# Four down stages of a two-layer hybrid block: product 4 copied by ScalarE with an adding DMA, squares added by DMAs, the short stage's weights loaded and split sooner

## The chip, the cores and the metric

The kernel runs on one core of a Trainium2 chip. Its engines each work through their own list of instructions in order: TensorE (PE, matrix products), VectorE (DVE), ScalarE (ACT), GpSimd (POOL) and SyncE (SP, which here only issues DMAs). POOL and ACT issue DMAs too. An instruction waits at the head of its engine's list until semaphores say that its operands are there. The metric is the device time of one execution in microseconds (us), as the median of several runs. The profile is of one execution, and its span is a little shorter than that execution's device time.

## The reference

Two layers of a hybrid transformer over 1024 tokens of width 1024, in float32. Layer 0 mixes tokens by a bidirectional retention (four heads, 256 context tokens ahead), layer 1 by a gated convolution of width 3. Each is followed by a SwiGLU feed-forward layer (hidden width 2816):

```python
hx = hx + g1 * yx                       # yx: retention or convolution, ends in a matmul by w_out
fx = modulate(rms_norm(hx, norm_ffn[i]), sh2, sc2)
hx = hx + g2 * swiglu(fx, ffn_w1[i], ffn_w3[i], ffn_w2[i])
...
return rms_norm(hx, final_norm)
```

Shifts, scales and gates (`sh`, `sc`, `g`) come from the conditioning vector. So each of the four sub-layers ends in the same pattern: a matrix product back to width 1024 (here called a down stage), times a gate, added to the residual stream `hx`, and then the root mean square of the new `hx` over its 1024 channels, which scales the input of what follows.

## The kernel before

Activations lie with channels on the 128 partitions: the stream is 8 channel tiles (`kt` 0 to 7) by 2 token blocks (`tb`) of 512 tokens, each a tile of 128x512. TensorE multiplies with a rounded operand type, so each operand is split in a high and a low part: `split` lets ScalarE copy and round (L132, or L127 with a sign) and VectorE subtract (L133, L128), and `mm3` makes three matmuls of it (L137, L138, L139).

The large products use Winograd's form of Strassen's algorithm: operands in 2x2 blocks, seven products instead of eight. A down stage, made by `down`, runs its seven products in the order 1, 5, 6, 3, 7, 4, 2. Each product is `nh` units, one for each pair of hidden tiles, and each unit is 4 output tiles by 3 matmuls. The stages are A (`o_run`, the retention's output, nh 8), B (first FFN, nh 11), C (the convolution's output, nh 4, called the short stage) and D (last FFN, nh 11, which also makes the final result).

- **Operands.** `operands(m)` runs three units ahead: it loads one tile of activations (L1110, from `x_d` in DRAM, where the stage before stored it), splits it, forms the weight sum of this product and splits that. `w_load` (L1090) loads half a weight tile on SP's queue; `w_add` (L1094) adds two weight tiles by an accumulating DMA on POOL's queue. First halves are loaded ahead of the stage, second halves in product 1, unit by unit.
- **Results.** At the end of a product, `finished` calls `update` for each of its 4 tiles. For products 1, 5 and 6 (`D_FIRST`), ScalarE copies the sum with the gate (L1142) and an accumulating DMA of POOL adds the residual (L1143). For products 3, 7, 4 and 2 VectorE adds to the tile that is there (L1146). `D_OUT` says which tile and token block a product belongs to; product 4 gives tiles 4 to 7 of the first block, to which `load_h` has loaded the residual on SP's queue (L1135) at the start of product 7.
- **Norm.** `complete` squares each finished tile (ScalarE, L1165 for a block's first, L264 for others), adds the square to the block's sum (VectorE, L265), and stores the tile for the next residual (L1169). `norm_steps` then gives the list of small pieces: `rstd` (TensorE's L270 sums over partitions, VectorE's chain L275 to L155 takes the reciprocal root), L288 puts it on a diagonal, L296 on TensorE spreads it, and the next stage's tiles are scaled by it (L1301).
- **Order.** `hooks` is a queue of small pieces of work. After each unit `unit_done` takes one or two out and runs them, so that their instructions land between units; `nothing` is an empty piece that ends the turn. The second block's norm is queued at the start of product 4 and the first block's at the stage's end, so that its steps run between the first units of the stage that follows.
- **Last stage.** In D, product 2 does its 256 first tokens, keeps the operands and does the other 256 after. ScalarE scales finished tiles by the final gain (L1415, `result_tile`) and TensorE turns them (L1409, `result_turn`).

A scheduler places instructions on each engine from this program's order, and pools of buffers (`up`, `tp`, `lp` and 8 PSUM banks) decide when a load or a copy may begin.

Of the kernel before, what the change touches and what calls it, by code (L numbers as in the profile page):

```python
# [14 lines left out]
AF = mybir.ActivationFunctionType  # L15
ALU = mybir.AluOpType
# [7 lines left out]
KT = D // P  # L24
# [28 lines left out]
def hybrid_kernel(ctx: ExitStack, tc: tile.TileContext, a: dict):  # L53
    nc = tc.nc
# [18 lines left out]
    def ttile():  # L73
        return tp.tile([P, 512], F32, tag="t", name="tt")
# [12 lines left out]
    def ttile2():  # L87
        return extra["l"].tile([P, 512], F32, tag="l", name="t2")
# [17 lines left out]
    hooks = deque()  # L106
# [115 lines left out]
    def until(ready):  # L222
        while not ready():
            hooks.popleft()()
# [82 lines left out]
    def in_parts(src):  # L307
        u = unit()
        split(u[:, 0], u[:, 1], src)
        return u  # L310
# [754 lines left out]
    H = {}  # L1065
# [5 lines left out]
    D_AHEAD = 3  # L1071
# [1 line left out]
    LATER = slice(0, TB // 2), slice(TB // 2, TB)  # L1073
    D_LOADS = 3

    D_FIRST = (1, 5, 6)

    def down(src, nh, w, gate, residual, order, consume, then=(), last=False):

# [6 lines left out]
        def w_load(k, half):  # L1086
            if k not in wr:
                wr[k] = raw()
            c = slice(half * 512, (half + 1) * 512)
            nc.sync.dma_start(wr[k][:, c], w[k][:, c])  # L1090

        def w_add(i):

            nc.gpsimd.dma_start(wr[i][:, 512:], w[nh + i][:, 512:], accum_op=ALU.add)  # L1094

        loaded = [0]

# [15 lines left out]
        def operands(m):  # L1113
            x_loads(m + 1, True)
            x_loads(m + 1 + D_LOADS)
            if m >= len(seq):
                return
            n, i = seq[m]
            xs[m] = in_parts(xl.pop(m))
            wa, wc = wr[i][:, :512], wr[i][:, 512:]  # L1120
            if n != 1:
                wb, wd = wr[nh + i][:, :512], wr[nh + i][:, 512:]
            if n == 6:
                nc.vector.tensor_sub(wc, wc, wa)
            if n in (3, 7):
                t = ttile()
                nc.vector.tensor_sub(t, wb if n == 3 else wd, wc)
            else:
                t = wa if n == 1 else {5: wc, 6: wc, 2: wb, 4: wd}[n]
            ws[m] = in_parts(t)  # L1130

        def load_h():
            for kt in range(4, KT):
                H[kt, order[0]] = ttile2()
                nc.sync.dma_start(H[kt, order[0]], residual(kt, order[0]))  # L1135

        def update(n, kt, tb, ps, t):

# [9 lines left out]
        def norm_steps(tb):  # L1148
            box = {}

            def diag():
                box["dg"] = rstd_diag(accs[tb], TB)

            def bank_of(i, step):
                if i == 0:
                    box["rb"] = spread(box["dg"], TB)
                step(box["rb"])

            return [diag, nothing] + [lambda i=i, f=f: bank_of(i, f) for i, f in enumerate(consume(tb))]

        def complete(kt, tb, t):
            h = H[kt, tb]
            if tb not in accs:
                accs[tb] = ttile()
                nc.scalar.activation(accs[tb], h, AF.Square)  # L1165
            else:
                sq_add(accs[tb][:, t], h[:, t], False, t.stop - t.start)
            if not last:
                nc.scalar.dma_start(h_d[kt][tb], h)  # L1169

        ahead = [lambda i=i: w_load(i, 0) for i in range(nh)]
        ahead[3:3] = [lambda: x_loads(D_LOADS)]
        ahead += [lambda m=m: operands(m) for m in range(D_AHEAD)]

        def step(ps, c, w, x, t, first, end):
            k = slice(c * P, (c + 1) * P)
# [2 lines left out]
        def run():  # L1179
            banks, kept = {}, []  # L1180

            def finished(n, c, ps, t):
                j, r = D_OUT[n]
                kt, tb = 4 * j + c, order[r]
                update(n, kt, tb, ps, t)
                if n in (3, 7, 2, 4):
                    complete(kt, tb, t)
                if last and n in (2, 4):
                    result_tile(kt, t)

            for m, (n, i) in enumerate(seq):
                which = "A" if n in (1, 6, 7, 4) else "B"
                if i == 0:
                    if n == 7:
                        load_h()
                    if n == 5:
                        until(lambda: src(2, nh - 1) is not None)
                    if n in (1, 5, 2):
                        banks[which] = [bank() for _ in range(4)]
                    if n == 4:  # L1200
                        hooks.extend(then[:1])
                        hooks.extend(norm_steps(order[1]))
                        hooks.extend(then[1:])
                    if n == 2 and last:
                        hooks.extend(
                            lambda kt=kt: result_turn(kt, LATER[0]) for kt in range(4, KT)
                        )
                if n == 1:
                    w_load(i, 1)
                    w_load(nh + i, 1)  # L1210
                    w_add(i)
                if n == 6:
                    w_load(nh + i, 0)
                until(lambda: m in ws)
                operands(m + D_AHEAD)
                w, x = ws.pop(m), xs.pop(m)
                t = TOKENS
                if last and n == 2:
                    kept.append((w, x))
                    t = LATER[0]  # L1220
                for c in range(4):
                    step(banks[which][c], c, w, x, t, n in (1, 5, 2) and i == 0, i == nh - 1)
                if i == nh - 1:
                    for c in range(4):
                        finished(n, c, banks[which][c], t)
                unit_done(2 if n in (1, 2, 4) or nh == 4 else 1)
            if last:
                flush()
                acc = accs[order[0]]
                for c in range(4):  # L1230
                    ps = bank()
                    for i, (w, x) in enumerate(kept):
                        step(ps, c, w, x, LATER[1], i == 0, i == nh - 1)
                    finished(2, c, ps, LATER[1])
                    if c == 0:
                        for kt in range(4):
                            result_turn(kt, LATER[0])
                        y = result_norm(acc, LATER[0])
                    if c == 1:
                        result_end(y, LATER[0])  # L1240
                        for kt in range(4, KT):
                            result_turn(kt, LATER[1])
                    if c > 1:
                        result_turn(c - 2, LATER[1])
                y = result_norm(acc, LATER[1])
                for c in (2, 3):
                    result_turn(c, LATER[1])
                result_end(y, LATER[1])
            else:
                hooks.extend(norm_steps(order[0]))  # L1250
# [398 lines left out]
```

## Time and profile before

| | us |
|---|---|
| median of 3 runs | 2626.91 (2619.53 to 2627.34) |
| profiled execution | 2628.3 |
| its span | 2626.4 |
| PE busy | 2565.5 (98%) |
| DVE busy | 1889.3 (72%) |
| ACT busy | 1235.6 (47%) |
| POOL busy | 323.7 (12%) |
| mean granted TensorE clock | 0.992 |

A row of a timeline gives start, duration, engine, line, operation, output and input, and in brackets how long the engine stood idle before it and what ended that. A row of a window gives its bounds and length, TensorE's busy time (and instructions), the granted clock (1.00 is full), the DMA engines' share and GB/s. A row of waits gives total, times and longest. Rows of one line give minimum, median and maximum in ns, and first and last start. A matmul's duration overlaps the next one's, so their pace is the distance between starts. Part 6 of the page gives, for each kind of DMA, the count, its size and the median time from issue to landing.

### The profile page before, as it was taken

The page shows a single profiled execution, that of the slowest core. Times are in us where ns is not written, and L with a number is a line of the kernel's source. Part 1 is how long each engine was busy: PE and PEld are TensorE (multiplying, and loading weights), DVE is VectorE, ACT ScalarE, POOL GpSimd, SP SyncE. Part 2 cuts the span into 40 slices and gives each one's busy share as a digit, 9 for nine tenths or more (in the row PEclk, how much of TensorE's full clock was granted, in tenths as well). Part 3 has the DMA queues.
Part 4 walks back from the last instruction along what each step waited for, and adds up shares of the span by engine and source line. Part 5 has one row for each costly group of instructions (what it writes and reads, how often), then busy time and mean ns, then how long its engine had stood idle before and what let it go on. Part 6 is the DMA issues. An engine that isn't in the chain of part 4 may idle for free.

```text
span 2626.4 us, 33369 instructions
## 1 busy us (share of the span) xinstructions
PE 2565.5 (98%) x11508; PEld 2099.9 (80%) x11508; DVE 1889.3 (72%) x3333; ACT 1235.6 (47%) x2239; POOL 323.7 (12%) x370
## 2 busy tenths in 40 slices
PE   8999999999989999999999999999999999999998
PEld 4788888887777787888887888788777888887888
DVE  4886766767887867777776767777688666655766
ACT  4653232447776545433333545533366333333544
POOL 1100222002332102000001100200112000002100
PEclk9999999999999999999999999999999999999999
DMA  9546233764569957444556945432685333329733
GB/s 328 203 149 220 92 124 128 260 216 132 182 217 279 272 157 161 135 157 153 181 187 214 276 138 172 91 100 98 181 240 103 117 104 112 109 89 299 199 88 117
DMA packets 218985, 445.12 MB, mean 169 GB/s; under 512 B 23104, under 2 KB 52928, under 8 KB 218816
## 3 DMA queue, kind: packets, MB, share of 16 engines
q1 hardware_dynamic: 149232, 297.94, 35.4%
q0 software_dynamic: 32864, 79.19, 12.4%
q10 hardware_dynamic: 36720, 65.86, 6.7%
q8 instruction: 91, 1.49, 0.2%
q14 instruction: 78, 0.64, 0.1%
HBM read 320.74 MB, written 109.58 MB: 164 GB/s over the span
## 4 chain that ended last, share of the span: by engine, by line
PE 86%; DVE 6%; DMA 5%; issue 2%; ACT 1%; SPq 0%; DVEq 0%; ACTq 0%
PE ps L137 28%; PE ps L138 28%; PE ps L139 27%; DVE u L133 2%; PE ps L237 1%; DMA tt<-x_d 1%; DMA tt<-os_d 1%; DMA tt<-g_d 1%; DVE u L675 1%; PE ps L947 0%; DVE kh L634 0%; PE ps L296 0%; DMA raw<-in_w_g 0%; DVE tt L265 0%; PE ps L270 0%
## 5 line engine op out<-in xcount | busy, mean ns | idle before, releaser
L137 PE MATMUL ps<-u 128*128 128x512 f32 (+1 forms) x3492 | 1363.7, 391 | 17.9 <-DVE u L133 8.5
L138 PE MATMUL ps<-u 128*128 128x512 f32 (+1 forms) x3492 | 1356.7, 389 | 2.1 <-DVE u L133 1.9
L139 PE MATMUL ps<-u 128*128 128x512 f32 (+1 forms) x3492 | 1355.9, 389 | 0.0
L137 PEld LDWEIGHTS ps<-u 128*128 128x128 f32 x3492 | 659.1, 189 | 162.5 <-ACT u L132 10.0
L138 PEld LDWEIGHTS ps<-u 128*128 128x128 f32 x3492 | 659.7, 189 | 137.7 <-DVE u L133 4.7
L139 PEld LDWEIGHTS ps<-u 128*128 128x128 f32 x3492 | 659.4, 189 | 135.1 <-issue 0.7
L132 ACT CAST u<-raw 128x512 fp32r<-128x512 f32 x622 | 375.5, 619 | 379.9 <-PE ps L139 234.3
L133 DVE TENSOR_TENSOR u<-raw,u 128x512 fp32r<-128x512 f32 x622 | 434.8, 711 | 60.2 <-ACT u L132 59.4
L133 DVE TENSOR_TENSOR u<-tt,u 128x512 fp32r<-128x512 f32 x358 | 242.2, 700 | 123.4 <-ACT u L132 121.4
L132 ACT CAST u<-tt 128x512 fp32r<-128x512 f32 x358 | 211.9, 620 | 206.0 <-DMA tt<-x_d 102.4
L443 ACT COPY tt<-ps 128x512 f32<-128x512 f32 x192 | 112.6, 587 | 251.8 <-PE ps L139 244.5
L128 DVE SCALAR_TENSOR_TENSOR u<-raw,u 128x512 fp32r<-128x512 f32 x168 | 114.9, 688 | 76.6 <-ACT u L127 76.4
L127 ACT ACTIVATE u<-raw 128x512 fp32r<-128x512 f32 x168 | 105.1, 632 | 88.2 <-PE ps L139 75.8
L1263 POOL DMA_DIRECT2D x_d<-tt x52 | 28.3, 544 | 837.6 <-DVE tt L1276 774.2
L456 DVE TENSOR_TENSOR tt<-tt,ps 128x512 f32<-128x512 f32 x64 | 43.8, 684 | 80.3 <-PE ps L139 80.2
L675 DVE SCALAR_TENSOR_TENSOR u<-ps,u 128x512 fp32r<-128x512 f32 x128 | 84.9, 684 | 20.8 <-ACT u L674 20.7
L624 POOL TENSOR_TENSOR u<-t,u 128x512 fp32r<-128x512 f32 x40 | 55.3, 1386 | 279.3 <-ACT u L623 269.9
L450 DVE TENSOR_TENSOR tt<-tt,ps 128x512 f32<-128x512 f32 x64 | 44.0, 687 | 61.8 <-ACT tt L443 58.4
L674 ACT ACTIVATE u<-ps 128x512 fp32r<-128x512 f32 x128 | 74.2, 598 | 28.8 <-PE ps L139 26.8
L1146 DVE SCALAR_TENSOR_TENSOR t<-ps,ada,t 128x512 f32<-128x512 f32 x48 | 33.9, 747 | 53.3 <-PE ps L139 52.0
L210 DVE SCALAR_TENSOR_TENSOR raw<-raw,c_row 128x512 f32<-128x512 f32 x84 | 55.2, 686 | 20.1 <-DMA raw<-in_ada_t 20.0
L446 DVE TENSOR_TENSOR tt<-tt,ps 128x512 f32<-128x512 f32 x64 | 43.8, 684 | 23.7 <-PE ps L139 23.7
(162 smaller groups left out, 2054.5 us busy)
## 6 DMA issues: line engine op xcount, KB each, us to landing
tt<-x_d SPq DMA_DIRECT2D x182, 256.0 KB, 4.6
raw<-in_w SPq DMA_DIRECT2D x88, 512.0 KB, 4.1
raw<-in_w SPq DMA_DIRECT2D x88, 256.0 KB, 5.4
raw<-in_ada_t SPq DMA_DIRECT2D x42, 512.0 KB, 5.2
x_d<-tt ACTq DMA_DIRECT2D x78, 256.0 KB, 2.3
t<-in_ada_t SPq DMA_DIRECT2D x76, 256.0 KB, 6.3
raw<-in_w_v SPq DMA_DIRECT2D x36, 512.0 KB, 4.7
x_d<-tt POOLq DMA_DIRECT2D x52, 256.0 KB, 2.7
```

What stands on the lines that cost most here:

```text
L127: nc.scalar.activation(dst_hi, src, AF.Copy, scale=-1.0)
L128: nc.vector.scalar_tensor_tensor(dst_lo, src, -1.0, dst_hi.bitcast(F32), op0=ALU.mult, op1=ALU.subtract)
L132: nc.scalar.copy(dst_hi, src)
L133: nc.vector.tensor_sub(dst_lo, src, dst_hi.bitcast(F32))
L137: nc.tensor.matmul(ps, w_hi, x_lo, start=first, stop=False, **kw)
L138: nc.tensor.matmul(ps, w_lo, x_hi, start=False, stop=False, **kw)
L139: nc.tensor.matmul(ps, w_hi, x_hi, start=False, stop=last, **kw)
L210: nc.vector.scalar_tensor_tensor(w[e], w[e], 1.0, c_row[:, k], op0=ALU.mult, op1=ALU.mult, accum_out=sums[:, e, ct : ct + 1],)
L443: nc.scalar.copy(m[p, n], ps)
L624: nc.gpsimd.tensor_sub(t[:, 1], v, t[:, 0].bitcast(F32))
L674: nc.scalar.activation(s[:, 0], st[d][m], AF.Copy, scale=f)
L675: nc.vector.scalar_tensor_tensor(s[:, 1], st[d][m], f, s[:, 0].bitcast(F32), op0=ALU.mult, op1=ALU.subtract,)
```

## The change

1. Product 4 joins `D_FIRST`: ScalarE copies its four sums with the gate and an accumulating DMA adds the residual. `load_h` is gone. Its tiles are completed not at the end of product 4 but in product 2, at its third unit; in D they are also scaled there, and their turns queued.
2. The first four tiles of a block are squared into four tiles. An accumulating DMA adds each pair, and `four` adds the two pairs by another one, at the last unit of product 7 (second block) and of product 2 (first block). The other four squares are added by VectorE as before.
3. `norm_steps` begins with one more `nothing`, so a norm starts one unit later.
4. In the short stage (nh 4) the second halves of the weights (`w_rest`) are loaded ahead of the stage instead of in product 1, and the weights of products 4 and 2 are split ahead of their units, in products 3 and 7 (`w_early`).

```diff
-    D_FIRST = (1, 5, 6)
+    D_FIRST = (1, 5, 6, 4)
...
+        def w_rest(i):
+            w_load(i, 1)
+            w_load(nh + i, 1)
+            w_add(i)
...
-            ws[m] = in_parts(t)
-
-        def load_h():
-            for kt in range(4, KT):
-                H[kt, order[0]] = ttile2()
-                nc.sync.dma_start(H[kt, order[0]], residual(kt, order[0]))
+            ws[m] = early.pop((n, i), None) or in_parts(t)
...
-            return [diag, nothing] + [lambda i=i, f=f: bank_of(i, f) for i, f in enumerate(consume(tb))]
+            return [nothing, diag, nothing] + [lambda i=i, f=f: bank_of(i, f) for i, f in enumerate(consume(tb))]
+
+        squares = {}
 
         def complete(kt, tb, t):
+
             h = H[kt, tb]
             if tb not in accs:
-                accs[tb] = ttile()
-                nc.scalar.activation(accs[tb], h, AF.Square)
+                sq = squares.setdefault(tb, {})
+                sq[kt] = ttile()
+                nc.scalar.activation(sq[kt], h, AF.Square)
+                if kt % 2:
+                    nc.gpsimd.dma_start(sq[kt - 1], sq[kt], accum_op=ALU.add)
             else:
                 sq_add(accs[tb][:, t], h[:, t], False, t.stop - t.start)
             if not last:
                 nc.scalar.dma_start(h_d[kt][tb], h)
 
+        def four(tb):
+            accs[tb], other = [squares[tb][kt] for kt in sorted(squares[tb]) if kt % 2 == 0]
+            nc.gpsimd.dma_start(accs[tb], other, accum_op=ALU.add)
...
-        ahead += [lambda m=m: operands(m) for m in range(D_AHEAD)]
+        for m in range(D_AHEAD):
+            ahead.append(lambda m=m: operands(m))
+            if nh == 4:
+                ahead.append(lambda m=m: w_rest(m))
+        if nh == 4:
+            ahead.append(lambda: w_rest(3))
+        early = {}
+
+        def w_early(n, i):
+            early[n, i] = in_parts(wr[nh + i][:, 512:] if n == 4 else wr[nh + i][:, :512])
...
-                if n in (3, 7, 2, 4):
+                if n in (3, 7, 2):
                     complete(kt, tb, t)
-                if last and n in (2, 4):
+                if last and n == 2:
                     result_tile(kt, t)
...
-                    if n == 7:
-                        load_h()
+                    if n in (3, 7) and nh == 4:
+                        k = 4 if n == 3 else 2
+                        hooks.extend(lambda i=i, k=k: w_early(k, i) for i in range(nh))
...
-                    if n == 2 and last:
-                        hooks.extend(
-                            lambda kt=kt: result_turn(kt, LATER[0]) for kt in range(4, KT)
-                        )
-                if n == 1:
-                    w_load(i, 1)
-                    w_load(nh + i, 1)
-                    w_add(i)
+                if n == 2 and i == 2:
+                    for kt in range(4, KT):
+                        complete(kt, order[0], TOKENS)
+                        if last:
+                            result_tile(kt, TOKENS)
+                            hooks.append(lambda kt=kt: result_turn(kt, LATER[0]))
+                if n in (7, 2) and i == nh - 1:
+                    four(order[0 if n == 2 else 1])
+                if n == 1 and nh > 4:
+                    w_rest(i)
```

In the changed kernel the activation load is L1115, the square L1169, the pairs' addition L1171, the addition of `four` L1179, the next stage's scaling L1325, the last stage's scaling L1439 and its turns L1433; L1090, L1142, L1143 and the lines before them keep their numbers.

How this moves instructions is shown at three places. The first is SP's list at the start of C: weight loads (`raw<-in_w_co`) and loads of activations (`tt<-x_d_...`, the digits behind `x_d` are the product less one and the pair). Before:

```order
L1090 DMA raw_16144<-in_w_co 128x512 x2
L1110 DMA tt_16147<-x_d_0_3_234 128x512
L1110 DMA tt_16149<-x_d_4_0_275 128x512
L1110 DMA tt_16151<-x_d_4_1_276 128x512
L1110 DMA tt_16153<-x_d_4_2_277 128x512
L1090 DMA raw_16174<-in_w_co 128x512 x2
L1090 DMA raw_16198<-in_w_co 128x512
L1090 DMA raw_16222<-in_w_co 128x512
L1090 DMA raw_16198<-in_w_co 128x512
L1090 DMA raw_16222<-in_w_co 128x512
L1110 DMA tt_16177<-x_d_4_3_278 128x512
```

And now:

```order
L1090 DMA raw_16071<-in_w_co 128x512
L1090 DMA raw_16075<-in_w_co 128x512
L1090 DMA raw_16071<-in_w_co 128x512
L1090 DMA raw_16075<-in_w_co 128x512
L1115 DMA tt_16159<-x_d_0_3_234 128x512
L1115 DMA tt_16161<-x_d_4_0_275 128x512
L1115 DMA tt_16163<-x_d_4_1_276 128x512
L1115 DMA tt_16165<-x_d_4_2_277 128x512
L1115 DMA tt_16185<-x_d_4_3_278 128x512
```

The six weight loads that stood between product 5's third and fourth activation tile stand ahead of all of them.

The second place is VectorE's list at the end of A, from the last square's addition to the diagonal (`rs_` names are the small tiles of the reciprocal root, `raw` the next stage's weights). Before, from the second of three rounds on:

```order
L151 TENSOR_TENSOR rs_u_9134<-rs_y_9126 128x4
L152 SCALAR_TENSOR_TENSOR rs_u_9134<-rs_u_9134,rs_v_9124 128x4
L155 SCALAR_TENSOR_TENSOR rs_y_9126<-rs_u_9134,rs_y_9126 128x4
L151 TENSOR_TENSOR rs_u_9138<-rs_y_9126 128x4
L152 SCALAR_TENSOR_TENSOR rs_u_9138<-rs_u_9138,rs_v_9124 128x4
L155 SCALAR_TENSOR_TENSOR rs_y_9126<-rs_u_9138,rs_y_9126 128x4
L288 TENSOR_SCALAR tt_9142<-ident_81,rs_y_9126 128x128 x4
```

And now:

```order
L151 TENSOR_TENSOR rs_u_9155<-rs_y_9147 128x4
L152 SCALAR_TENSOR_TENSOR rs_u_9155<-rs_u_9155,rs_v_9145 128x4
L155 SCALAR_TENSOR_TENSOR rs_y_9147<-rs_u_9155,rs_y_9147 128x4
L128 SCALAR_TENSOR_TENSOR u_9220<-raw_9098,u_9220 128x512
L151 TENSOR_TENSOR rs_u_9159<-rs_y_9147 128x4
L396 TENSOR_TENSOR raw_9098<-raw_9098,raw_8687 128x512
L152 SCALAR_TENSOR_TENSOR rs_u_9159<-rs_u_9159,rs_v_9145 128x4
L398 TENSOR_TENSOR raw_8687<-raw_9098 128x512
L155 SCALAR_TENSOR_TENSOR rs_y_9147<-rs_u_9159,rs_y_9147 128x4
L400 TENSOR_TENSOR raw_8687<-raw_8687,raw_9098 128x512
L288 TENSOR_SCALAR tt_9163<-ident_81,rs_y_9147 128x128 x4
```

Four full-width rows of the next stage's weights stand between the last round of the chain and the diagonal.

The third place is D. TensorE's list in product 2 (`ps` are its four sums, `t2` a finished tile that is turned) had, at the end of its first unit:

```order
L139 MATMUL ps_21676<-u_21596,u_21599 128x256
L1409 MATMUL ps_21697<-ident_81,t2_21120 128x128
L1409 MATMUL ps_21699<-ident_81,t2_21120 128x128
L137 MATMUL ps_21673<-u_21616,u_21619 128x256
L138 MATMUL ps_21673<-u_21616,u_21619 128x256
```

The same turn now stands at the end of the third unit:

```order
L139 MATMUL ps_21661<-u_21628,u_21631 128x256
L1433 MATMUL ps_21736<-ident_81,t2_21646 128x128
L1433 MATMUL ps_21738<-ident_81,t2_21646 128x128
L137 MATMUL ps_21658<-u_21664,u_21667 128x256
L138 MATMUL ps_21658<-u_21664,u_21667 128x256
```

And ScalarE's list, which gives that tile its scale (L1439), now reads:

```order
L1142 ACTIVATE t2_21655<-ps_20090,ada_1_5_97 128x512
L132 CAST u_21747<-raw_20236 128x512
L132 CAST u_21768<-tt_21682 128x512
L132 CAST u_21771<-raw_20260 128x512
L1169 ACTIVATE tt_21702<-t2_21646 128x512
L1169 ACTIVATE tt_21705<-t2_21649 128x512
L1439 ACTIVATE t2_21646<-t2_21646,cols_75 128x512
L1439 ACTIVATE t2_21649<-t2_21649,cols_75 128x512
L1169 ACTIVATE tt_21709<-t2_21652 128x512
L1169 ACTIVATE tt_21712<-t2_21655 128x512
```

The turn moved two units down TensorE's list, and the scale it needs stands behind the squares of two tiles, whose residuals arrive by DMA.

## The prediction

> **What bounds the kernel now.** I read the page's busy table and its chain of waits first.
>
> ```profile
> PE 2565.5 (98%) x11508; PEld 2099.9 (80%) x11508; DVE 1889.3 (72%) x3333; ACT 1235.6 (47%) x2239; POOL 323.7 (12%) x370
> PE 86%; DVE 6%; DMA 5%; issue 2%; ACT 1%; SPq 0%; DVEq 0%; ACTq 0%
> ```
>
> TensorE is busy for 98% and the chain runs through it. Rows taken off VectorE are worth nothing in themselves; what can be won is time in which TensorE stands still or runs slowly. So I read TensorE's waits, then its timeline at the ends and starts of the four down stages: A (8 pairs of hidden tiles, attention output, ends near 1009 us), B (11 pairs, first FFN), C (4 pairs, the short stage after the convolution) and D (11 pairs, the last).
>
> ```profile
> PE ps L270 <- DVE tt L265: 7.4, 4, 3.6
> 1004.67 0.39 PE L139 MATMUL ps<-u 128*128 128x512 f32 x1
> 1008.75 0.39 PE L139 MATMUL ps<-u 128*128 128x512 f32 x1
> 1012.76 1.39 PE L270 MATMUL ps<-ones,tt 128*128 128x1 f32 x8 [3.62 <-DVE tt L265]
> 1014.00 0.77 PE L137 MATMUL ps<-u 128*128 128x512 f32 x1
> 1014.58 0.63 PE L138 MATMUL ps<-u 128*128 128x512 f32 x1
> 1018.84 0.63 PE L139 MATMUL ps<-u 128*128 128x512 f32 x1
> 1013.00:1019.00 6.00, 6.00 (x20) 0.53 0.00 0
> ```
>
> The two 1004-1008 rows are 18 matmuls apart: 0.227 us each, so one unit of a product (12 matmuls) is 2.72 us. At A's end the sum of squares reaches L270 3.62 us late, and what follows is slow: from 1014.58 to 1018.84 ten steps of 0.426 us. The window's granted clock is 0.53. The twelve matmuls behind the stall cost 12 x 0.20 = 2.4 us more, so this one wait costs 6.0 us.
>
> C shows the same at its start and its end.
>
> ```profile
> 1899.01 0.39 PE L139 MATMUL ps<-u 128*128 128x512 f32 x1
> 1902.43 0.47 PE L137 MATMUL ps<-u 128*128 128x512 f32 x1 [3.03 <-DVE u L133]
> 1903.00:1908.00 5.00, 5.00 (x15) 0.66 0.92 326
> 1963.51 0.94 PE L137 MATMUL ps<-u 128*128 128x512 f32 x3 [2.45 <-DVE u L133]
> 1966.13 0.39 PE L139 MATMUL ps<-u 128*128 128x512 f32 x1
> 1975.19 1.27 PE L270 MATMUL ps<-ones,tt 128*128 128x1 f32 x8 [1.81 <-DVE tt L265]
> 1973.00:1980.00 7.00, 5.19 (x20) 0.76 0.12 43
> ```
>
> The start loses 3.03 us and then 5 x (1 - 0.66) = 1.7 us of clock: 4.7. Between 1966.13 and L270 at 1975.19 TensorE does one unit (2.72) in 9.1 us.
>
> **The change part by part.** *Work moved off VectorE.* Product 4's 16 rows L1146 go to 16 of ScalarE's L1142, each with an adding DMA L1143; 24 of the 52 full-width additions L265 go to DMAs; 16 loads L1135 go from SP.
>
> ```profile
> L1146 DVE SCALAR_TENSOR_TENSOR t<-ps,ada,t x48: 736/750/752, 935.7 to 2581.2; 128x512 f32<-128x512 f32 x48
> L265 DVE TENSOR_TENSOR tt<-tt x67: 412/681/693, 5.1 to 2617.1; 128x512 f32<-128x512 f32 x52, 128x256 f32<-128x256 f32 x15
> L1142 ACT ACTIVATE t<-ps,ada x32: 671/682/695, 899.3 to 2489.3; 128x512 f32<-128x512 f32 x32
> L1143 POOL DMA_DIRECT2D t<-h_d x24: 868/1201/1850, 1495.7 to 2490.3; - x24
> DMA to landing us min/median/max: 4.7/7.8/11.6
> ```
>
> That is 16 x 0.75 + 24 x 0.68 = 28.3 us less on VectorE, 16 x 0.68 = 10.9 more on ScalarE, and 40 more issues of 0.9 to 1.9 us on GpSimd; the last row is the landing of all 48 L1143. Under TensorE's 2.72 us per unit all of it is covered except at the stage ends; without cover ScalarE's four copies would be 2.7 us per stage. What counts is that each sum now waits for landings where it waited for VectorE.
>
> *A's end.* The norm starts one unit (2.72 us) later and four of its eight squares are summed earlier, so half of the VectorE work behind the last unit is gone. The 3.62 us stall and its 2.4 go: +6.0. But the rsqrt chain behind L270 gets company.
>
> ```profile
> 1014.18 0.16 DVE L275 TENSOR_SCALAR rs_v<-ps 128x4 f32<-128x4 f32 x1 [1.48 <-PE ps L270]
> 1016.55 0.87 DVE L288 TENSOR_SCALAR tt<-ident,rs_y 128x128 f32<-128x128 f32 x4
> L396 DVE TENSOR_TENSOR raw<-raw x56: 678/691/694, 1028.8 to 2368.9; 128x512 f32<-128x512 f32 x56
> ```
>
> Before, the chain takes 1017.42 - 1014.18 = 3.24 us. Afterwards four weight rows of the next stage (L128, L396, L398, L400; about 0.69 each) stand inside it: 6.0 us. It begins 1.42 us after L270 starts, so L296 has its operand 7.4 us after that start. TensorE reaches L296 after 1.24 (1014.00 - 1012.76) and one unit: 3.96. Idle 3.4 us. The slow clock after it I take at 8 matmuls, 1.6 us (between none and A's 12, 2.4). A: 6.0 - 3.4 - 1.6 = **+1.0**, from -0.8 (12 slow matmuls, and up to 1 us for the next stage's sums of operands, which start one unit later) to +6.0 (the rows are done before the chain begins).
>
> *B's end.* The rest of the L270 waits, 7.4 - 3.62 - 1.81 = 2.0, is B's and D's, near half each; B's goes: **+0.9** (0 to 1).
>
> *C's start.* On SP the loads of the first operands stand behind six weight loads.
>
> ```profile
> 1884.47 4.86 SPq L1090 DMA_DIRECT2D raw<-in_w_co  x6
> 1887.79 0.58 POOL L1263 DMA_DIRECT2D x_d<-tt  x1 [20.72 <-DVE tt L1276]
> DMA to landing us min/median/max: 6.0/6.0/6.0
> x_d<-tt POOLq DMA_DIRECT2D x52, 256.0 KB, 2.7
> tt<-x_d SPq DMA_DIRECT2D x182, 256.0 KB, 4.6
> 1893.87 4.31 SPq L1110 DMA_DIRECT2D tt<-x_d  x8
> 1900.94 0.62 ACT L132 CAST u<-tt 128x512 fp32r<-128x512 f32 x1 [8.14 <-DMA tt<-x_d]
> ```
>
> The landing row is that of the 1887.79 store: 6.0 us among the weight transfers, against the page's median of 2.7. Its load goes out at 1893.87 and is used at 1900.94, 7.1 later, against 4.6. The change puts all sixteen weight loads ahead of the operand loads and of that store, as soon as their buffers are free. At the medians the cast stands at 1887.8 + 2.7 + 4.6 = 1895.1 and the split operands 1.3 to 1.9 later, under 1899.01 (the cast and one subtraction, or the weights' too). **+4.7**; 0 if the transfers still meet.
>
> *C's end.* The square of tile 7 waits for the landing of its residual, an addition within pairs and one of both pairs by DMA follow, then four L265 (2.7), then L270. For such an adding DMA between tiles the nearest rows are L1330's.
>
> ```profile
> L1330 POOL DMA_DIRECT2D t<-tt x12: 874/1098/1358, 1022.6 to 1986.7; - x12
> DMA to landing us min/median/max: 3.3/5.3/7.3
> ```
>
> Counted from product 4's end: issue of the fourth DMA 1.9 (an estimate from three more issues of 0.87 to 1.2 behind the first), landing 10, square 0.6, two DMAs of 3.3 to 5.3, additions 2.7: L270 after 22 to 26. Now product 4 ends at 1966.36 - 4 x 2.72 - 2.45 = 1953.0, and L270 comes 22.2 later. Of these TensorE works 13.6 (five units); afterwards 16.3, since one unit more stands ahead of L270. It loses 8.6 now, 5.7 to 9.7 then: -1 to +3. I take **+1.0**, the middle.
>
> *D's end.* In D the four tiles finished early are turned by TensorE inside product 2.
>
> ```profile
> 2579.18 2.79 DVE L1146 SCALAR_TENSOR_TENSOR t<-ps,ada,t 128x512 f32<-128x512 f32 x4 [0.82 <-PE ps L139]
> 2580.68 0.72 ACT L1415 ACTIVATE t<-t,cols 128x512 f32<-128x512 f32 x1
> 2581.02 0.28 PE L137 MATMUL ps<-u 128*128 128x256 f32 x1
> 2582.45 0.38 PE L1409 MATMUL ps<-ident,t 128*128 128x128 f32 x2
> L1143 POOL DMA_DIRECT2D t<-h_d x4: 872/1358/1843, 2488.6 to 2490.3; - x4
> DMA to landing us min/median/max: 6.3/8.8/11.0
> ```
>
> Now the first turn is ready 1.4 us after product 2 begins. Afterwards it stands three units in (2581.02 + 3 x 1.44 = 2585.3; a half-width unit is 2582.45 - 2581.02), and waits for ScalarE's scaling L1439, which stands behind the squares L1169 of tiles 4 and 5, hence behind the landing of tile 5's residual. That DMA can be issued at 2580.8. D's last set of four landed 6.3 to 11.0 after issue, with a median of 8.8, so its second lay between 6.3 and 8.8. That gives 2587.1 to 2589.6, with square and scaling (0.63, as ScalarE's other squares, and 0.72) 2588.4 to 2590.9: a stall of 3.1 to 5.6 us. I take 3.4, near the fast end because no weights are loaded beside it any more, and 1.8 for the clock (half of 3.6 us at half speed). The cost is **-5.2** (-8 to 0, if landings are quick). The casts behind the squares on ScalarE are needed only from the seventh unit on (2589.7 plus the stall).
>
> On the clock there is a rule. The Trainium skill (TensorE: Matmul & The Clock Gate, "What's actually happening") puts the half clock after at least one idle window of about 3.4 us and lets the window run free. The rows partly disagree: 3.03 us was enough at 1902 and 1.81 at 1975, but 2.45 at 1963 was not followed by a slow row. By the page's figure as a threshold, an estimate, both new stalls would just escape the slow clock, and the sum would be better by 1.6 + 1.8.
>
> Sum: 1.0 + 0.9 + 4.7 + 1.0 - 5.2 = **2.4 us** faster. The profiled execution took 2628.3 (span 2626.4), so 2625.9; it stood 1.4 above the median of 2626.91 (three runs, 2619.53 to 2627.34), so **2624.5**.
>
> **The rivals.** *The gain comes whole.* D's turns are not late (landings under 5 us; for it, L1143's fastest row in the trace is 4.7 us; against it, that was a first of four), and A's weight rows slip out of the chain's way: 2.4 + 5.2 + 5.0 = 12.6 us, 2614.3.
>
> *It ends slower, through ScalarE's queue.* Each stage's square stands in ScalarE's order ahead of the casts for later units. If fourth landings exceed about 10.5 us (the quoted set's slowest is 11.0), these casts miss their units in A and B as well, each 1 us and 1.6 of clock; with D at -8, C's end at -1 and A's chain at -0.8 the sum is 4.7 - 8 - 1 - 0.8 - 5.2 = -10.3: 2637.2. For it: DMA landings spread widely; against: long stages have five units' time.
>
> *The start of C does not move*, since buffers for the early weights come free late or the store is still slow: 2.4 - 4.7 = -2.3, 2629.2. For it: that store waits for the last product of the stage before, which stays.
>
> **How the numbers follow.** About 0.3% (7.9 us) is what a measurement of this kernel can tell from no change. Forecast 0.40, whole gain 0.32, slower 0.13, unmoved start 0.15. Forecast and unmoved start lie within 0.3%, but the forecast's edge crosses 2619.0: faster 0.33, same 0.54, slower 0.13. Bounds added (-0.8, 0, 0, -1, -8 against 6, 1, 4.7, 3, 0) give 2636.7 and 2612.2; all slow ends together are unlikely, so the range is 2612 to 2634, and the forecast's own 2618 to 2630.
>
> **What would show it.** After: no L270 wait in A and B; an L296 wait of about 3 us in A on L288; no idle before C's first L137, with the store landing in about 3 us; a wait of 3 to 5 us of TensorE on L1439 in D with clock near 0.5 behind it. No such wait in D, or none in A at L296, proves my sum too low; ScalarE casts late behind L1169 in A or B prove it too high.

## The result, and the profile after

The changed kernel is slower: 2645.32 us in the median of 6 runs (2641.26 to 2648.22) against 2626.74 (2619.53 to 2631.17) of the kernel before on the same chip, a ratio of 1.0074 with a 95% interval of 1.0063 to 1.0084. I had forecast 2624.5 and a range up to 2634.

The busy table and TensorE's waits of the changed kernel:

```profile
PE 2566.7 (97%) x11508; PEld 2101.0 (79%) x11508; DVE 1868.3 (71%) x3293; ACT 1243.5 (47%) x2255; POOL 359.1 (14%) x410
PE ps L270 <- DVE tt L265: 15.3, 3, 11.3
PE ps L137 <- DVE t L1146: 4.7, 1, 4.7
PE ps L296 <- DVE tt L288: 4.0, 2, 2.5
PE ps L1433 <- ACT t L1439: 3.6, 1, 3.6
```

VectorE has 21 us less to do and 40 instructions fewer, as intended, and TensorE's work is the same. But L270, the norm's first matmul, now waits 15.3 us in all where it waited 7.4, once for 11.3 us, and two waits are new: L137 on L1146 and L1433 on L1439.

To see where, I compared the start of the same unit of TensorE in the two traces (changed less before; its movement within a stage is what the stage gained or lost). Ahead of A the changed kernel's profiled execution is 6.9 us early, in work that the change does not touch; at the end it is 18.1 us late. So 25 us are lost from A on in this pair of executions, and 18.6 between the medians. Each line is read from one execution of either kernel, and the stretches between the stages, which the change hardly touches, move by 2.4 and 1.7 us as well.

| stretch | difference, us, from and to | effect, us | predicted |
|---|---|---|---|
| A's end | -6.9 to -8.4 | gain 1.6 | gain 1.0 |
| between A and B's end | -8.4 to -6.0 | loss 2.4 | nothing |
| B's end | -6.0 to -1.6 | loss 4.4 | gain 0.9 |
| C's start | -1.6 to -5.9 | gain 4.3 | gain 4.7 |
| C's products 7 and 4 | -5.9 to 0.0 | loss 5.9 | nothing |
| C's end | 0.0 to +10.8 | loss 10.8 | gain 1.0 |
| between C and D's end | +10.8 to +12.6 | loss 1.7 | nothing |
| D's end | +12.6 to +18.1 | loss 5.6 | loss 5.2 |

Three terms came out near their size: A's end, C's start and D's end. Three did not (B's end, C's products 7 and 4, C's end), and they have one thing in common. These are rows of SP and GpSimd around the norms of the changed kernel's C, and for each addition of squares its time from issue to landing (the first landing row is that of the last addition at 1929.61, the second of the pair additions at 1965.07 and 1967.40, the third of B's last addition at 1630.34):

```profile
1929.52 2.08 SPq L369 DMA_DIRECT2D raw<-in_w  x4
1929.61 0.87 POOL L1179 DMA_DIRECT2D tt<-tt  x1 [3.94 <-issue]
DMA to landing us min/median/max: 9.8/9.8/9.8
1964.78 2.83 SPq L369 DMA_DIRECT2D raw<-in_w  x4
1965.07 0.87 POOL L1171 DMA_DIRECT2D tt<-tt  x1 [7.50 <-DVE u L133]
1967.40 0.88 POOL L1171 DMA_DIRECT2D tt<-tt  x1 [1.45 <-ACT tt L264]
DMA to landing us min/median/max: 9.7/10.2/10.7
DMA to landing us min/median/max: 10.5/10.5/10.5
```

I had taken 3.3 to 5.3 us for such an addition. Over all 16 pair additions the median is 4.2, but each time that the next stage's first four weight loads (512 KB each) go out beside an addition, it takes 9.7 to 10.7. At C's end four stores of finished tiles are under way as well. What waits behind them shows on VectorE and TensorE:

```profile
1939.49 0.69 DVE L265 TENSOR_TENSOR tt<-tt 128x512 f32<-128x512 f32 x1 [5.66 <-DMA tt<-tt]
1940.10 0.74 DVE L1146 SCALAR_TENSOR_TENSOR t<-ps,ada,t 128x512 f32<-128x512 f32 x1
1940.89 0.66 PE L137 MATMUL ps<-u 128*128 128x512 f32 x1 [4.69 <-DVE t L1146]
1982.04 2.29 DVE L265 TENSOR_TENSOR tt<-tt 128x512 f32<-128x512 f32 x3 [14.39 <-DMA tt<-tt]
1986.00:1992.00 6.00, 6.00 (x18) 0.50 0.32 60
```

In product 7, L265 stands ahead of the last L1146 in VectorE's list; until that has read its PSUM bank, TensorE can't begin the next product. At C's end TensorE waits 11.3 us, and then runs for 6 us at half clock.

That the loads go out at just these moments is no accident, as SP's own waits show (first B's end, then C's product 7, then C's end):

```profile
SPq L1115 <- DMA tt<-tt: 10.0, 1, 10.0
SPq L1115 <- DMA tt<-tt: 8.9, 2, 8.2
SPq L369 <- DMA h_d<-t: 24.3, 4, 23.0
```

The load of an activation tile (L1115) needs a small buffer, and the squares now hold these until the pair addition has landed. SP stands there for 8 to 10 us with the weight loads behind it, and lets them out in the moment in which the last addition starts. At C's end it is another wait: in the compiled program each of the four weight loads waits on a semaphore that it shares with the store of one of product 4's four tiles, whose completion has moved into product 2. Before, these loads went out from 1949.06 to 1960.54 (the last issue ends there), two of them ahead of the squares of product 4's tiles and two behind, and none of the additions was a DMA that could meet them:

```profile
1949.06 11.47 SPq L369 DMA_DIRECT2D raw<-in_w  x4
```

So the theory after the result: the squares' own DMAs cost the time, since they meet bulk loads which the change itself has bunched up. The rivals: product 4's late completion costs it, or the early splits, whose buffers are missing elsewhere.

### The profile page after: what moved, and what is told of

The parts are those of the page before. It is cut to its first block, busy times and chain, and to the rows that moved or that the text cites. A ratio compares the mean times of both kernels' runs of the same rounds, so it can differ in the third digit from the quotient of the medians.

```text
span 2644.5 us, 33428 instructions
## 1 busy us (share of the span) xinstructions
PE 2566.7 (97%) x11508; PEld 2101.0 (79%) x11508; DVE 1868.3 (71%) x3293; ACT 1243.5 (47%) x2255; POOL 359.1 (14%) x410
## 5 line engine op out<-in xcount | busy, mean ns | idle before, releaser
L137 PE MATMUL ps<-u 128*128 128x512 f32 (+1 forms) x3492 | 1363.5, 391 | 24.8 <-DVE u L133 10.3
L137 PEld LDWEIGHTS ps<-u 128*128 128x128 f32 x3492 | 659.0, 189 | 169.2 <-ACT u L132 11.0
L456 DVE TENSOR_TENSOR tt<-tt,ps 128x512 f32<-128x512 f32 x64 | 43.9, 686 | 81.2 <-PE ps L139 81.1
L450 DVE TENSOR_TENSOR tt<-tt,ps 128x512 f32<-128x512 f32 x64 | 44.0, 687 | 62.2 <-ACT tt L443 59.2
L1143 POOL DMA_DIRECT2D t<-h_d x36 | 32.1, 1208 | 250.1 <-ACT t L1142 249.9
L981 POOL TENSOR_TENSOR raw<-tt,raw 128x512 f32<-128x512 f32 x16 | 23.5, 1472 | 293.6 <-DVE tt L446 181.5
```

The source lines that it names most:

```text
L137: nc.tensor.matmul(ps, w_hi, x_lo, start=first, stop=False, **kw)
```

## The experiments

Each ratio is to the kernel before, run beside it on the same chip (medians of 2624.0, 2624.1 and 2625.1 us in three sets of runs; in the first comparison it was 2626.7).

| kernel | median, us | ratio (95%) |
|---|---|---|
| changed kernel | 2645.32 | 1.0074 (1.0063 to 1.0084) |
| squares by VectorE | 2623.82 | 0.9997 (0.9984 to 1.0011) |
| product 4 by VectorE | 2630.73 | 1.0021 (1.0011 to 1.0031) |
| short stage's weights late | 2649.31 | 1.0094 (1.0074 to 1.0114) |
| D's turns later | 2637.45 | 1.0041 (1.0026 to 1.0056) |
| squares in the weights' buffers | 2639.35 | 1.0057 (1.0043 to 1.0071) |
| last addition by VectorE | 2635.64 | 1.0042 (1.0028 to 1.0056) |
| product 4's stores by GpSimd | 2649.22 | 1.0087 (1.0071 to 1.0104) |
| the same in the short stage alone | 2638.23 | 1.0052 (1.0039 to 1.0065) |
| squares by VectorE and D's turns later | 2619.27 | 0.9978 (0.9969 to 0.9987) |
| the same without the empty piece | 2619.85 | 0.9981 (0.9972 to 0.9990) |
| early weights and the empty piece | 2620.01 | 0.9980 (0.9970 to 0.9990) |
| early weights alone | 2617.67 | 0.9970 (0.9959 to 0.9981) |

**One part undone at a time.** First the squares:

```diff
-                sq = squares.setdefault(tb, {})
-                sq[kt] = ttile()
-                nc.scalar.activation(sq[kt], h, AF.Square)
-                if kt % 2:
-                    nc.gpsimd.dma_start(sq[kt - 1], sq[kt], accum_op=ALU.add)
+                accs[tb] = ttile()
+                nc.scalar.activation(accs[tb], h, AF.Square)
...
-                if n in (7, 2) and i == nh - 1:
-                    four(order[0 if n == 2 else 1])
```

> The changed kernel with the squares of all tiles added by VectorE again; product 4, the early weights and the extra empty piece stay. Theory 1, the squares' own adding DMAs cost the time (they land 10 us after issue where the next stage's four 512 KB weight loads go out with them: B's end 4.4 us, C's product 7 5.9, C's end about 9): about 19 us less than the changed kernel, 2626 (2622 to 2631). Theory 2, the late completion of product 4's tiles costs it: nothing but VectorE's 16 us of additions come back, 2643 to 2647. Theory 3, the early splits hold buffers that the next stage's weights need: C's end stays late, 2635.

Measured: 2623.82, the time of the kernel before; against the changed kernel's median (of another set of runs) 21.5 us came back. Theory 1 holds for the bulk. Theory 3 falls, and so does theory 2 as the only cause; whether product 4 has a share is the next run's question. In this kernel's trace TensorE's waits from C's start to its end are:

```profile
PE ps L137 <- ACT u L132: 2.5, 1, 2.5
PE ps L138 <- DVE u L133: 1.9, 1, 1.9
PE ps L296 <- DVE tt L288: 1.6, 1, 1.6
PE ps L137 <- DVE u L133: 1.4, 1, 1.4
```

The waits of 11.3 and 4.7 us are gone. Next, product 4 (the load of its residual and its `complete` are put back where they were):

```diff
-    D_FIRST = (1, 5, 6, 4)
+    D_FIRST = (1, 5, 6)
...
-                if n in (3, 7, 2):
+                if n in (3, 7, 2, 4):
                     complete(kt, tb, t)
...
-                if n == 2 and i == 2:
-                    for kt in range(4, KT):
-                        complete(kt, order[0], TOKENS)
...
```

> The changed kernel with product 4 added by VectorE again (its residual loaded in product 7, its tiles completed at its end); squares by DMA, early weights and the extra empty piece stay. Theory 1: D's 5.5 us and the part of C's end come back that the stores of product 4's tiles cost by standing ahead of the weight loads; the slow additions in C's product 7 stay: 2630 to 2637. Theory 2: nearly all comes back, 2625 to 2628. Theory 3: only D's part, 2640.

2630.73, within theory 1's expectation, at its lower edge. D's wait on L1439 is gone. So is nearly all of the wait at C's end, though the squares are still added by DMAs: the pair additions there go out before three of the four weight loads and land in 5.0 and 5.8 us. What is left is C's product 7, where L137 waits for the row of VectorE that answers to L1146 (L1151 in this kernel). The rows of C, from the slowest of this kernel's ten executions:

```profile
PE ps L270 <- DVE tt L265: 1.7, 1, 1.7
DMA to landing us min/median/max: 5.0/5.4/5.8
PE ps L137 <- DVE t L1151: 7.1, 2, 6.7
```

So C's end needs both parts, the additions by DMA and product 4's late completion. This kernel with the squares by VectorE too is the table's "early weights and the empty piece". With it, four kernels that all have those two tell the parts apart. The squares by DMA cost 0.77% with product 4 late (1.0074 against 0.9997) and 0.41% without (1.0021 against 0.9980); the late product 4 costs 0.53% with the squares by DMA and 0.17% without. Some 9 us are paid only where both are (each ratio's interval reaches 0.1% to either side or a little more). Then the short stage's weights:

```diff
-        for m in range(D_AHEAD):
-            ahead.append(lambda m=m: operands(m))
-            if nh == 4:
-                ahead.append(lambda m=m: w_rest(m))
-        if nh == 4:
-            ahead.append(lambda: w_rest(3))
+        ahead += [lambda m=m: operands(m) for m in range(D_AHEAD)]
...
-                    if n in (3, 7) and nh == 4:
-                        k = 4 if n == 3 else 2
-                        hooks.extend(lambda i=i, k=k: w_early(k, i) for i in range(nh))
...
-                if n == 1 and nh > 4:
+                if n == 1:
                     w_rest(i)
```

> The changed kernel with the short stage's weights loaded and split as before. Theories 1 and 2: C's start loses its 4.3 us again and the end stays late: 2648 to 2651. Theory 3: C's start loses 4.3 and C's end wins about 11: 2638 to 2640.

2649.31: this part was a gain of some 4 us, though the two intervals overlap, and C's long wait stays without it (10.8 us at L270). The last of the four moves D's turns only:

```diff
-                            hooks.append(lambda kt=kt: result_turn(kt, LATER[0]))
+                if last and n == 2 and i == 6:
+                    hooks.extend(lambda kt=kt: result_turn(kt, LATER[0]) for kt in range(4, KT))
```

> The changed kernel with one thing moved: in D the turns of tiles 4 to 7 are queued four units later, at the seventh unit of product 2, when their scaling is done. If D's 5 to 6 us are TensorE waiting for that scaling and the slow clock behind it: 2639 to 2641, and no wait on L1439's tiles. If the casts behind the squares in ScalarE's queue are what is late, the loss stays: 2644 to 2646.

2637.45, some 2 us better than expected: the move is worth 7.9 us between the medians (the two kernels were timed in different sets). TensorE waits nowhere in D on the scaling any more. In D the casts behind the squares were not what was late.

This kernel also shows how much of B's loss is the one execution's. In three kernels whose code in B is that of the changed kernel (this one, the one with the weights late and, below, the one with product 4's stores by GpSimd in the short stage alone) the last addition is as slow, 9.6 to 9.9 us, but B's L270 waits 0.6 to 1.4 us instead of 2.9, and B's end is 2.4 to 3.2 us shorter. So the change costs 1 to 2 us at B's end rather than 4.4.

**Why the additions are slow.** The wait for small buffers was tried by giving the squares others:

```diff
-                sq[kt] = ttile()
+                if kt % 2 == 0:
+                    both = raw()
+                    sq[kt], sq[kt + 1] = both[:, :512], both[:, 512:]
```

> The changed kernel with one thing else: the four tiles of squares lie in two of the large buffers of the weights' pool, not in four of the small tiles' pool, so that SP's next load of activations does not wait for the landing of a pair addition to get its buffer. Theory 1a: SP stands there until the pair addition lands and then sends the next stage's four weight loads out together with the last addition, which so lands in 10 us instead of 3 to 5; without that wait the last additions of B's end and of C's product 7 land in 3 to 5 us, 10 us come back, and C's end stays (its pair additions meet other loads): 2635 (2633 to 2638). Theory 1b, such additions are slow there whatever SP does: 2643 to 2647.

2639.35: 6 of the 10 us that I expected came back, and the time lies between the two forecasts. SP no longer waits for a pair addition, and B's end loses nothing more (TensorE's only wait there is 0.5 us at L296, and the last addition, at 8.1 us, is early enough). But in C's product 7 the weight loads now go out earlier and meet the pair additions. SP's and GpSimd's rows of this kernel (L1173 is the pair addition, L1181 the last one), with the landing row of the pair additions:

```profile
1913.80 10.56 SPq L369 DMA_DIRECT2D raw<-in_w  x4
1917.80 0.87 POOL L1173 DMA_DIRECT2D raw<-raw  x1 [5.51 <-ACT raw L1171]
1920.18 0.88 POOL L1173 DMA_DIRECT2D raw<-raw  x1 [1.50 <-ACT raw L1171]
DMA to landing us min/median/max: 8.6/9.0/9.3
PE ps L137 <- DVE t L1146: 4.6, 1, 4.6
```

The last addition then takes 4.3 us instead of 9.8, but it starts as much later, and TensorE's wait is unchanged. The buffer decided when the loads go out, but an addition is slow where it meets them, be it the pairs' or the last one. Stores of finished tiles are under way there too; the run with the stores moved in the short stage, below, has such stores beside its pair additions and no weight loads. Taking the last addition off the DMA queues goes further:

```diff
-            nc.gpsimd.dma_start(accs[tb], other, accum_op=ALU.add)
+            nc.vector.tensor_add(accs[tb], accs[tb], other)
```

> The changed kernel with the addition of the two pairs by VectorE (one row of 0.7 us) and only the pairs by DMA. Theory 1, both forms: B's end and C's product 7 lose nothing more, C's end 4 us less: 2632 to 2636. If the pair additions or the landings of the residuals are what is late in B and in product 7, little changes: 2641 to 2645.

2635.64, as expected: product 7 loses nothing more, and at B's end TensorE waits 0.5 us in all. C's end is 3 us shorter but keeps a wait of 9.5 us at L270, since its pair additions meet the loads (9.8 and 12.0 us). For C's end the stores were moved to another queue, first in all stages:

```diff
-                nc.scalar.dma_start(h_d[kt][tb], h)
+                q = nc.gpsimd if tb == order[0] and kt >= 4 else nc.scalar
+                q.dma_start(h_d[kt][tb], h)
```

> The changed kernel with one thing else: the stores of product 4's four tiles go out on GpSimd's queue. In the changed kernel the next stage's four weight loads in C wait for these stores, although they don't read them, and go out at 1964.8 to 1967.3 together with both pair additions, which land in 9.7 and 10.7 us. If that is the cause of C's end, the loads go out between 1950 and 1962 as before the change, the pair additions land in 4 to 6, the wait at C's L270 falls from 11.3 us to about 6: 2639 (2637 to 2641). If the chain of landings is too long by itself, 2644 to 2647.

2649.22, slower by 4 instead of faster by 6. C's end did what was expected: pair additions in 5.5 and 6.0 us, and a wait of 6.0 at L270. The loss is in A, where GpSimd's list now holds the fourth residual (L1143 at 994.90) behind stores (L1176) that wait for their own tiles' landings; TensorE's wait behind it follows as the last row:

```profile
985.09 0.88 POOL L1143 DMA_DIRECT2D t<-in_xT  x1 [0.31 <-ACT t L1142]
992.93 0.57 POOL L1176 DMA_DIRECT2D h_d<-t  x1 [4.86 <-DMA t<-in_xT]
994.90 0.94 POOL L1143 DMA_DIRECT2D t<-in_xT  x1
1003.78 0.77 PE L137 MATMUL ps<-u 128*128 128x512 f32 x1 [5.87 <-DVE u L133]
```

So the same edit was made for the short stage alone:

```diff
-                nc.scalar.dma_start(h_d[kt][tb], h)
+                q = nc.gpsimd if nh == 4 and tb == order[0] and kt >= 4 else nc.scalar
+                q.dma_start(h_d[kt][tb], h)
```

> The changed kernel with product 4's four tiles stored over GpSimd's queue in the short stage alone. If the former run lost its time in A, where GpSimd's list held the fourth residual back behind these stores, A is now as in the changed kernel and what is left is C's end: pair additions in 5 to 6 us, the wait at L270 near 6 instead of 11.3, 2639 to 2641. If the short stage too loses by the stores in GpSimd's list, 2643 to 2647.

2638.23, 7 us under the changed kernel. The weight loads go out at 1941.00, the pair additions at 1964.66 have only each other and some stores of 256 KB beside them and land in 5.7 and 6.6 us:

```profile
1941.00 2.72 SPq L369 DMA_DIRECT2D raw<-in_w  x4
1964.66 1.82 POOL L1171 DMA_DIRECT2D tt<-tt  x2
DMA to landing us min/median/max: 5.7/6.1/6.6
PE ps L270 <- DVE tt L265: 7.9, 1, 7.9
```

The wait at L270 falls from 11.3 to 7.9, not to the expected 6: here the fourth residual stands behind stores too (issued at 1959.43 against 1956.70 in the changed kernel, although this execution is 1.1 us ahead there). Within the traces C's end is 4.6 us shorter than in the changed kernel. The meeting of loads and additions is thus shown as the cause of a good part of C's end. The rest, a chain of three landings where there were VectorE rows, hangs on the late start of that chain: with product 4 completed at its own end, above, the same chain leaves a wait of 1.7 us.

**A version that beats both.** With squares on VectorE and D's turns late together:

> The squares by VectorE and D's turns at the seventh unit, together; product 4 by ScalarE and the early weights stay. If the two causes add: 2623.8 less 5 to 7, 2617 to 2619, 0.2 to 0.3% under the kernel before. If without D's wait VectorE's end work becomes the limit in D, 2621 to 2624.

2619.27, 0.9978 of the kernel before; by the ratios the turns are worth 5 us here (0.9997 against 0.9978). The same without the extra empty piece:

```diff
-            return [nothing, diag, nothing] + ...
+            return [diag, nothing] + ...
```

> Squares by VectorE, D's turns at the seventh unit, product 4 by ScalarE, early weights, without the extra empty piece. Against 2619.3 with it: if the piece is worth 2 to 3 us in A, 2621 to 2623; if with less work on VectorE at the stage's end the wait at L270 is short anyway, 2617 to 2620.

2619.85: the piece makes no difference. And the kernel before with the early weights and that piece, and with the early weights alone (the diff of the weights above, turned round):

> The kernel before with the early weights and the one extra empty piece ahead of each norm; product 4 and all squares by VectorE. If the extra piece is worth A's 6.0 us wait less the late chain (3 to 5), and about nothing elsewhere: 1 to 3 us under the early weights alone, 2616 to 2619. If it only moves the wait from L270 to L296: as the early weights alone.

> The kernel before with the short stage's early weights alone. If C's start is worth its 4.3 us by itself and C's end is not made worse: 0.9983 of the kernel before, 4 to 5 us less, 2619 to 2620. If the buffers that the early splits hold delay the next stage's weights, or C's end takes the gain back: 2622 to 2626.

2620.01 and 2617.67. The early weights alone give the lowest median, 7.4 us under the kernel before beside it, though its interval overlaps the others'. Product 4 on ScalarE and the extra piece add nothing that these runs can tell. In the early weights' trace C's start is about 5 us shorter than before and the rest of C 1 to 2. The weight loads on SP are now over before the activations:

```profile
1860.25 5.92 SPq L1090 DMA_DIRECT2D raw<-in_w_co  x5
1880.05 20.09 SPq L1115 DMA_DIRECT2D tt<-x_d  x15
```

I expected 4 to 5 us of it. Where the rest comes from is not shown: the early loads and the early splits were not run apart, and ahead of A's end, where this edit changes nothing, the two traces already differ by 5 us.

## Why the prediction was wrong, point by point

**C's start: right.** Predicted 4.7, measured 4.3, and by the predicted way: in the changed kernel TensorE has no wait there, and the store on which the first operands hang lands in 2.3 us, where it took 6.0 before.

```profile
1886.78 0.58 POOL L1287 DMA_DIRECT2D x_d<-tt  x1 [19.89 <-DVE tt L1300]
DMA to landing us min/median/max: 2.3/2.3/2.3
```

**A's end: right in kind and nearly in size.** The 3.62 us at L270 are gone and L296 waits instead, 2.54 us where I had 3.4:

```profile
1004.96 1.05 PE L270 MATMUL ps<-ones,tt 128*128 128x1 f32 x8
1011.41 1.13 PE L296 MATMUL ps<-tt,ones 128*128 128x512 f32 x2 [2.54 <-DVE tt L288]
1012.97 0.63 PE L139 MATMUL ps<-u 128*128 128x512 f32 x1
1012.00:1016.00 4.00, 4.00 (x12) 0.58 0.06 10
```

That the exchange is worth next to nothing is also what the runs without the extra piece say. The 1.6 us of the table are the whole of stage A and not this term alone; they hold a loss of 1.1 us that belongs to a rival, below.

**D's end: right.** Predicted a stall of 3.4 and 1.8 of clock; in the changed kernel:

```profile
2600.40 0.63 ACT L1169 ACTIVATE tt<-t 128x512 f32<-128x512 f32 x1 [2.50 <-DMA t<-h_d]
2600.94 1.32 ACT L1439 ACTIVATE t<-t,cols 128x512 f32<-128x512 f32 x2
2601.69 0.44 PE L1433 MATMUL ps<-ident,t 128*128 128x128 f32 x2 [3.60 <-ACT t L1439]
2604.00:2610.00 6.00, 6.00 (x42) 0.78 0.45 79
```

ScalarE stood until tile 5's residual had landed, and TensorE on ScalarE's scaling. Moving the turns took the wait away, 5 us with the squares on VectorE and 7.9 with the squares by DMA.

**C's end: the step that failed.** It is the term "two DMAs of 3.3 to 5.3" for the additions of squares, taken from L1330's landings, which gave L270 22 to 26 us after product 4's end and a gain of 1.0 as the middle. In the changed kernel product 4 ends at 1953.0. These are tile 7's square and L270:

```profile
1965.20 0.61 ACT L1169 ACTIVATE tt<-t 128x512 f32<-128x512 f32 x1
1985.52 1.87 PE L270 MATMUL ps<-ones,tt 128*128 128x1 f32 x8 [11.29 <-DVE tt L265]
```

Up to the square the sum was right: it ends 12.8 us after product 4, where 1.9 + 10 + 0.6 makes 12.5 (in parts by luck: the residual landed sooner than I had taken, at 1960.70, and ScalarE came to the squares later). Then the second pair addition goes out at 1967.40 and lands after 10.7 us, where I had 3.3 to 5.3. The last addition takes 3.4, within my range, and the four L265 3.4 instead of 2.7. L270 starts 32.5 us after product 4's end, and C's end lost 10.8. The rows of L1330 run while no loads are under way. The row I should have used stood in my own text: a store of the same size that took 6.0 us among weight loads instead of 2.7. I also kept the next stage's weight loads at their old place, though the change moved the stores with whose semaphores they wait.

**B's end and C's product 7: terms missing.** I gave B a gain of 0.9 for the wait at L270 and costed the last addition in product 7 at nothing ("all of it is covered except at the stage ends"). Its landing of 9.8 us holds VectorE's list, and with it a PSUM bank: 4.7 us of TensorE's time and some slow clock behind it. B's L270 waits 2.9 us in this execution and 0.6 to 1.4 in the other three, from 0.9: the gain did not come. I had written that each sum "now waits for landings where it waited for VectorE", but for the sums of squares I priced that wait at C's end alone.

**The rival on the slower side** had a sum of 2637.2, by casts that miss their units behind ScalarE's squares. Its mechanism is there, but small. In A a square stands 3.1 us for its residual, and TensorE waits for the operands whose casts stand behind it; in C a cast behind the squares is late as well:

```profile
990.41 0.63 ACT L1169 ACTIVATE tt<-t 128x512 f32<-128x512 f32 x1 [3.08 <-DMA t<-in_xT]
992.42 0.70 PE L137 MATMUL ps<-u 128*128 128x512 f32 x2 [1.17 <-DVE u L133]
1966.37 0.50 PE L137 MATMUL ps<-u 128*128 128x512 f32 x1 [2.47 <-ACT u L132]
```

The wait in A is the 1 us that the rival had named; the one in C replaces a wait of 2.45 us at the same place before. In B and D no cast is late. So the rival had the sign and a mechanism worth about 1 us, but not the one that cost the time, and its chance of 0.13 was too low: the change added 24 DMAs and 16 residual landings to paths that end at TensorE, and I let one price stand for all.

**On the clock,** the changed kernel adds two rows. After A's 2.54 us idle the granted clock was 0.58, and after D's 3.60 it was 0.78 over 6 us. The Trainium skill (TensorE: Matmul & The Clock Gate, "What's actually happening") asks for at least one idle window of about 3.4 us. The 2.54 us speak against that as a threshold for one idle stretch, as the 1.81 us before did; the measurement decides, and the slow clock belonged into both terms. The rows give no other threshold either: behind the 2.45 us before, and behind 1.74 us at 978.76 in the changed kernel, the granted clock stayed at 1.00.

## What to carry to other kernels

An addition moved from an engine to a DMA is not off the path: its price is its landing under the load of that moment, so look up what is sent out on the other queues beside it, and take the price from a row with that load. A buffer held until such a landing also moves every transfer that stands behind the next user of that buffer, which can bring about the very meeting that makes it slow. When a change has several parts, each is worth a run of its own: here one of four carried the whole gain, and two others together cost more than it gave. Two parts can also cost more together than apart, as the squares and product 4 did, so the runs without either one and without both are needed to tell.

## What the runs showed of the hardware

The same addition of 256 KB between two tiles took 3.3 us at D's end, with hardly any other traffic, and 8.1 to 12.0 us with four 512 KB loads sent beside it, mostly with some stores under way too; with such stores and no loads it took 5.7 and 6.6. A plain store of that size went from 2.7 to 6.0 us. I had not expected a factor of three. And idle stretches of TensorE as short as 1.8 and 2.5 us were followed by some 3 us at half clock, so that a wait of 2 to 4 us cost 1.3 to 2.4 us more. Others of 1.7 and 2.5 us were not.
